# A gate projection moved into the first stage's weight tiles, and a list scheduler that keeps to one TensorE tile size

## The chip, the cores and the metric

The kernel runs on one core of a Trainium2 chip. The metric is the device time of one execution in microseconds (us); the time of a kernel is the median of its runs. The engines are TensorE (PE), VectorE (DVE), ScalarE (ACT), GpSimd (POOL), and SyncE (SP), which here does nothing but issue DMAs. In a profile's row, L62 means line 62 of the kernel; lines 62, 65, 68, 74, 77, 84 and 90 are those of small helpers (matmul, transpose, activation, scalar-tensor-tensor, tensor-tensor, copy, DMA), so a row is told by its tile names.

## What is computed

One layer of a diffusion backbone, on 512 latent tokens and a prefix of 256 context tokens, width 1024, in fp32:

```
mod = silu(c) @ w_mod + b_mod
sh1, sc1, g1, sh2, sc2, g2 = split(mod, 6)
p_lat = modulate(rmsnorm(x, norm1_g), sh1, sc1) @ w_in
p_ctx = modulate(rmsnorm(ctx, norm1_g), sh1c, sc1c) @ w_in
y = token_mixers(p_lat, p_ctx, ...)
x = x + g1 * (y @ w_out)
x = x + g2 * (relu(modulate(rmsnorm(x, norm2_g), sh2, sc2) @ w_mlp1) ** 2 @ w_mlp2)
out = rmsnorm(x, final_g)
```

`mod` has six parts of 1024 columns each, so `w_mod` is 1024 x 6144. The first two (sh1, sc1) are needed before anything else; the third, g1, the gate of the mixers' output, is needed only when `y @ w_out` is added to x. The mixers are a Mamba-2 scan (16 heads) and a gated delta rule (8 heads) in both directions; the latter inverts triangular blocks.

## The kernel before, in words

**Stage 0** (lines 220 to 355, pools `stage0` and `m0`). Eight tiles `wm` of 128 x 2048, one for each 128 rows of `w_mod`, take its first 2048 columns in two halves (`wm_load`, line 232, 512 KB each). `modrow` (line 313) multiplies them by the silu of the conditioning vectors; `silp` is padded to 32 columns, so each product uses a 128 x 32 tile of the PE array, and four of them, with four different column groups, stand side by side:

```
314          for i in range(4):
315              c0 = DM * (i // 2) + 512 * half + 256 * (i % 2)
316              mm(mps[half][32 * i:32 * i + 32, :], silp[:, k, :], wm[k][:, c0:c0 + 256], k == 0, k == KB - 1)
```

The results (`mp`) become the columns with which `hmod` (line 301) modulates the normalized and transposed x (`xtp`, `xtq`, `xT`); it leaves them as a high part `hH` and a low part `hL`.

**Projections** (`proj`, line 390). `w_in` is read in blocks of 128 columns: `sm` (small parts), then k0 g0 q0 k1 q1 k2 and so on. A block is loaded into a staging tile `st` (two buffers, `W.load`), split by ACT into `wH` and by POOL into `wL` (`W.split`, two buffers each), and multiplied with `hH` and `hL` into a PSUM tile `pl` (latent, 512 columns) and, where needed, `pc` (context, 256). Behind each block stand convolutions on ACT and DVE. `post_sm` (line 495) turns block `sm` into decay rows (`smt`, `la`, `acp`, `gcol`, `rowp`, `va`, `rowsD`), which the delta rule's four inversions (`inverse`, line 684; their products are `kk`, `qk`, `z`, `y`) read back.

**The gate** (lines 857 to 873, pool `mods`, opened behind the projection's pools). 16 tiles `mg` of 128 x 512, with three buffers, take the third 1024 columns of `w_mod` (256 KB each); two products follow each load into `gatep`, the bias `gb` is added, and four small DMAs store the row in `gD`.

**The order of the work.** The code is traced once; `_Graph` (from line 1430) knows each instruction's dependencies and a modelled duration, and `run` (line 1550) is a list scheduler. Each engine takes, of its ready instructions, the one with the lowest key, and the key is almost entirely the place in the traced code; `_keep` (line 1705) then fixes that order on every engine, SP's queue included. A PE instruction whose tile size differs from the one before is charged a little more:

```
1608              p, k = heapq.heappop(now[e])
...
1621                  if shape and shape[0] != self.shape[k][0]:
1622                      d += 45.0
```

So an instruction stands in a fixed place on its engine, and where its data come later than the model thought, everything behind it on that engine waits.

Behind the inversions come the scans (from 400 us on), the output projection (from 680 us) and the MLP (from 790 us).

Of the kernel before, what the change touches and what calls it, by code (L numbers as in the profile page):

```python
# [9 lines left out]
F32 = mybir.dt.float32  # L10
F32R = mybir.dt.float32r
AF = mybir.ActivationFunctionType
ALU = mybir.AluOpType
# [3 lines left out]
P = 128  # L17
DM = 1024
KB = DM // P
# [19 lines left out]
def tile_hybrid_ssd_gdn_dit_block(  # L39
# [6 lines left out]
    ACT, DVE, POOL, PE, SP = nc.scalar, nc.vector, nc.gpsimd, nc.tensor, nc.sync  # L46
# [3 lines left out]
    def pool(name, bufs=1, side=None, space=None, rw=None):  # L50
        kw = {}
        if side:
            kw["side"] = side
        if space:
            kw["space"] = space
        if rw:
            kw["reuse_waits"] = rw
        st = ctx.enter_context(ExitStack())
        return st.enter_context(tc.tile_pool(name=name, bufs=bufs, **kw)), st.close

    def mm(o, lhsT, rhs, start=True, stop=True):
        PE.matmul(o, lhsT=lhsT, rhs=rhs, start=start, stop=stop)  # L62
# [13 lines left out]
    def tt(o, a, b, op, eng=None):  # L76
        (eng or DVE).tensor_tensor(out=o, in0=a, in1=b, op=op)  # L77
# [11 lines left out]
    def dma(o, i, q=None):  # L89
        (q or SP).dma_start(out=o, in_=i)  # L90
# [210 lines left out]
    def hmod(k):  # L301
        if k % 2:
            act(xT[:, k, 0:LAT], xT[:, k, 0:LAT], AF.Identity, scale=Gc[:, k, 0:1], bias=modc[:, k, 0:1])
        else:
            ts(xT[:, k, 0:LAT], xT[:, k, 0:LAT], Gc[:, k, 0:1], ALU.mult, modc[:, k, 0:1], ALU.add)
        ts(xT[:, k, LAT:TOK], xT[:, k, LAT:TOK], Gc[:, k, 1:2], ALU.mult, modc[:, k, 1:2], ALU.add)
        cast(hH[:, k, :], xT[:, k, :])
        tt(hL[:, k, :], xT[:, k, :], hH[:, k, :].bitcast(F32), ALU.subtract, DVE)
# [42 lines left out]
    modcols(1)  # L351
    for k in range(4, KB):
        hmod(k)
    close_s0()
    close_m0()

# [497 lines left out]
                dma(gD[idx - 2:idx - 1, c0 - idx * DM:c0 - idx * DM + MW], br)  # L854
        done.add(f"mods{idxs[-1]}")

    md, close_md = pool("mods", side="right", rw="tile")
    gb = md.tile([P, 256], F32, name="gb")
    POOL.memset(gb, 0.0)
    for j in range(4):  # L860
        dma(gb[32 * j:32 * j + 1, :], b_mod[:, 2 * DM + 256 * j:2 * DM + 256 * j + 256])
    gp = kqt([P, 256], "gatep")
    for k in range(KB):
        for half in range(2):
            w = md.tile([P, 512], F32, tag="mw", bufs=3, name=f"mg{k}_{half}")
            c0 = 2 * DM + 512 * half
            dma(w, w_md[P * k:P * k + P, c0:c0 + 512])
            for j in range(2):
                q = 32 * (2 * half + j)
                mm(gp[q:q + 32, :], silp[:, k, :], w[:, 256 * j:256 * j + 256], k == 0, k == KB - 1)  # L870
    tt(gb, gp, gb, ALU.add)
    for j in range(4):
        dma(gD[0:1, 256 * j:256 * j + 256], gb[32 * j:32 * j + 1, :])
    go(stream(N1, D["rate"]))
    for b in range(4):
        go(inverse(b))
# [199 lines left out]

    play("mD3", "g7")
    flush()
    close_md()
    close_cw()  # L1080
    close_iw()
    bx["sd"], close_sd = pool("ssd", side="right", rw="tile")
# [34 lines left out]
    W = Weights(order)  # L1117
# [277 lines left out]
_WINDOW = 3413.4  # L1395
_SLACK = (0.0, 100.0, 100.0, 100.0, 0.0)
_LANES = 8
_MIX = 1.2e9
_STRETCH = 1.0

# [12 lines left out]
class _Graph:  # L1413
# [136 lines left out]
    def run(self, key):  # L1550
# [37 lines left out]
        while done < n:  # L1588
# [15 lines left out]
            if not now[e]:  # L1604
                if soon[e]:
                    heapq.heappush(events, (soon[e][0][0], 0, e))
                continue
            p, k = heapq.heappop(now[e])
            if self.dma[k] and len(landed) >= _LANES and landed[-_LANES] > t:
                heapq.heappush(soon[e], (landed[-_LANES] + 30.0, p, k))  # L1610
                heapq.heappush(events, (t, 0, e))
                continue
# [6 lines left out]
            elif e == 0:  # L1619
                d = self.gap[k]  # L1620
                if shape and shape[0] != self.shape[k][0]:
                    d += 45.0
                elif shape and shape != self.shape[k] and shape[2] and self.shape[k][2]:
                    d *= 0.5
                shape = self.shape[k]
# [119 lines left out]
```

## Time and profile before

| | |
|---|---|
| median of 3 runs | 1162.48 us (1159.12 to 1164.63) |
| the profiled execution | 1160.29 us, span 1158.6 us |
| PE busy | 1091.5 us, 94% of the span |
| DVE, ACT, POOL busy | 721.4, 604.0, 456.0 us |
| mean granted PE clock | 0.978 |

The profiled execution lies 2.2 us below the median. The span is the time from its first to its last instruction. PE's matmuls are pipelined: what one of them costs is read from the starts of neighbours, not from its own length.

### The profile page before, as it was taken

To read this page: it belongs to the slowest core of one execution; us is meant where nothing else is said; L and a number is where in the kernel's file an instruction comes from. 1 tells how busy PE (TensorE), PEld (TensorE's weight loads), DVE (VectorE), ACT (ScalarE), POOL (GpSimd) and SP (SyncE) were. 2 spreads that over 40 slices of the span, in tenths; PEclk is the share of its full clock that TensorE was granted. 3 is DMA by queue.
4 is the path that set the end of the run, shared out by engine and by line. 5 is a ranking of instruction groups with operands and counts; after the bars stand their busy time and mean duration, and the time that the engine had idled before them with its cause. 6 is when DMAs were issued, how large, how long until landed. Compare 5 with 4: busy or idle time off the path is not lost.

```text
span 1158.6 us, 19228 instructions
## 1 busy us (share of the span) xinstructions
PE 1091.5 (94%) x7120; PEld 885.4 (76%) x7120; DVE 721.4 (62%) x1402; ACT 604.0 (52%) x1419; POOL 456.0 (39%) x386
## 2 busy tenths in 40 slices
PE   5799998998989999999999989999999999999997
PEld 2458877787868777788878868777777888888885
DVE  3775699897979557578766777878673022444023
ACT  4647656648364577578886674125333122444133
POOL 1216444442331332222322254433545445555462
PEclk9899999999999999999999989998999999999999
DMA  9577746686564694745372277743443333333332
GB/s 313 182 198 200 229 146 185 195 227 170 157 163 146 154 347 104 267 123 207 103 273 73 92 282 237 227 136 100 137 146 109 92 107 93 91 103 98 91 104 96
DMA packets 189334, 188.44 MB, mean 163 GB/s; under 512 B 41548, under 2 KB 140153, under 8 KB 189241
## 3 DMA queue, kind: packets, MB, share of 16 engines
q1 hardware_dynamic: 188336, 186.04, 52.6%
q8 instruction: 56, 0.92, 0.3%
q10 hardware_dynamic: 905, 1.18, 0.3%
q14 instruction: 37, 0.30, 0.1%
HBM read 151.45 MB, written 35.73 MB: 162 GB/s over the span
## 4 chain that ended last, share of the span: by engine, by line
PE 70%; DVE 11%; ACT 8%; DMA 6%; issue 3%; SPq 1%; POOL 0%; ACTq 0%; DVEq 0%; POOLq 0%
PE m1p L62 15%; PE m2a L62 15%; PE wo0a L62 4%; PE wo1a L62 3%; PE pl_x L62 3%; PE pl_v L62 3%; PE pl_g L62 2%; PE yp L62 2%; PE op L62 2%; PE pc_v L62 2%; DMA st_q<-in_w_in_dram 2%; PE pp L62 2%; PE pl_z L62 2%; PE up L62 2%; PE pc_x L62 2%
## 5 line engine op out<-in xcount | busy, mean ns | idle before, releaser
L77 POOL TENSOR_TENSOR wL_m<-st_m,wH_m 128x512 fp32r<-128x512 f32 x128 | 177.4, 1405 | 186.6 <-ACT wH_m L68 177.1
L68 ACT ACTIVATE wH_m<-st_m 128x512 fp32r<-128x512 f32 x128 | 77.1, 625 | 187.0 <-PE m2a L62 111.0
L62 PE MATMUL m1p<-h2hL,wH_m 128*128 128x512 f32 (+1 forms) x272 | 104.5, 384 | 1.6 <-DVE h2hL L77 1.5
L62 PE MATMUL m1p<-h2hH,wH_m 128*128 128x512 f32 (+1 forms) x272 | 103.6, 383 | 2.5 <-ACT rl L68 2.0
L62 PE MATMUL m1p<-h2hH,wL_m 128*128 128x512 f32 (+1 forms) x272 | 103.1, 380 | 0.0
L62 PE MATMUL m2a<-wL_m,aH 128*128 128x512 f32 x256 | 99.4, 389 | 0.0
L62 PE MATMUL m2a<-wH_m,aL 128*128 128x512 f32 x256 | 99.4, 389 | 0.0
L62 PE MATMUL m2a<-wH_m,aH 128*128 128x512 f32 x256 | 98.9, 389 | 0.0
L77 DVE TENSOR_TENSOR rtmp<-m2a,g2r 128x512 f32<-128x512 f32 x16 | 10.7, 683 | 140.1 <-PE m2a L62 140.0
L77 DVE TENSOR_TENSOR rl<-rl 128x512 f32<-128x512 f32 x32 | 47.5, 1484 | 51.8 <-ACT rl L68 51.5
L62 PEld LDWEIGHTS m1p<-h2hH,wH_m 128*128 128x128 f32 x272 | 51.8, 191 | 14.0 <-ACT rl L68 4.0
L77 POOL TENSOR_TENSOR wL_wo<-st_wo,wH_wo 128x512 fp32r<-128x512 f32 x32 | 45.2, 1433 | 41.1 <-ACT wH_wo L68 35.4
L74 DVE SCALAR_TENSOR_TENSOR macc<-mw,sil,macc 128x256 f32<-128x256 f32 x84 | 56.4, 671 | 7.2 <-DMA mw<-in_w_mod_dram 5.4
L62 PEld LDWEIGHTS m1p<-h2hL,wH_m 128*128 128x128 f32 x272 | 52.1, 191 | 11.5 <-DVE h2hL L77 2.4
L77 DVE TENSOR_TENSOR TD<-YD,ND 112x30 f32<-112x30 f32 (+14 forms) x120 | 59.6, 497 | 0.9
L62 PEld LDWEIGHTS m1p<-h2hH,wL_m 128*128 128x128 f32 x272 | 52.2, 192 | 9.4
L62 PEld LDWEIGHTS m2a<-wH_m,aH 128*128 128x128 f32 x256 | 48.0, 188 | 10.1
L62 PEld LDWEIGHTS m2a<-wL_m,aH 128*128 128x128 f32 x256 | 48.0, 188 | 10.0
L62 PEld LDWEIGHTS m2a<-wH_m,aL 128*128 128x128 f32 x256 | 48.0, 188 | 9.9
L77 DVE TENSOR_TENSOR YD<-YD,TD 112x30 f32<-112x30 f32 (+14 forms) x120 | 54.5, 454 | 0.9
L665 POOL TENSOR_SCALAR_AFFINE_SELECT rw<-rw 128x512 f32<-128x512 f32 x32 | 24.0, 764 | 64.7 <-ACT er L68 60.6
L68 ACT ACTIVATE wH_wo<-st_wo 128x512 fp32r<-128x512 f32 x32 | 18.5, 623 | 50.0 <-PE wo0a L62 21.6
(496 smaller groups left out, 3224.2 us busy)
## 6 DMA issues: line engine op xcount, KB each, us to landing
st_m<-in_w_mlp_dram SPq DMA_DIRECT2D x64, 512.0 KB
wm<-in_w_mod_dram SPq DMA_DIRECT2D x16, 512.0 KB
rw<-rowsD SPq DMA_DIRECT2D x16, 512.0 KB
st_wo<-in_w_out_dram SPq DMA_DIRECT2D x16, 512.0 KB
mw<-in_w_mod_dram SPq DMA_DIRECT2D x16, 512.0 KB
Ys<-invF SPq DMA_DIRECT2D x8, 768.0 KB
st_k<-in_w_in_dram SPq DMA_DIRECT2D x8, 512.0 KB
st_g<-in_w_in_dram SPq DMA_DIRECT2D x8, 512.0 KB
```

The source lines that it names most:

```text
L62: PE.matmul(o, lhsT=lhsT, rhs=rhs, start=start, stop=stop)
L68: ACT.activation(out=o, in_=i, func=f, **kw)
L74: (eng or DVE).scalar_tensor_tensor(out=o, in0=a, scalar=s, in1=b, op0=op0, op1=op1)
L77: (eng or DVE).tensor_tensor(out=o, in0=a, in1=b, op=op)
L665: POOL.affine_select(out=rw[:, d_], in_=rw[:, d_], pattern=[[0, n], [pat, P]], compare_op=ALU.is_ge, fill=NEG, base=0, channel_multiplier=cm_)
```

## The change

Three parts. The gate's products move to the end of stage 0: its weights are loaded into the columns 0 to 1023 of the `wm` tiles, once the products of both halves with the tile are done, in eight loads of 512 KB, with four products behind each; the pool `mods` and the `mg` tiles are gone. `W.load(2)`, the load of block g0, is called ahead of the gate's loads. And the list scheduler, when the PE instruction it is about to take has another tile size than the one before, looks through the 12 lowest keys for a ready one of the same size and takes that instead (`_NEAR` is so large that it never excludes one); a switch is charged 95 instead of 45.

```diff
@@ -351,6 +351,20 @@
     modcols(1)
     for k in range(4, KB):
         hmod(k)
+
+    gb = s0.tile([P, 256], F32, name="gb")
+    POOL.memset(gb, 0.0)
+    gp = mxt([P, 256], "gatep", m0)
+    for j in range(4):
+        dma(gb[32 * j:32 * j + 1, :], b_mod[:, 2 * DM + 256 * j:2 * DM + 256 * j + 256])
+    W.load(2)
+    for k in range(KB):
+        dma(wm[k][:, 0:DM], w_md[P * k:P * k + P, 2 * DM:3 * DM])
+        for j in range(4):
+            mm(gp[32 * j:32 * j + 32, :], silp[:, k, :], wm[k][:, 256 * j:256 * j + 256], k == 0, k == KB - 1)
+    tt(gb, gp, gb, ALU.add)
+    for j in range(4):
+        dma(gD[0:1, 256 * j:256 * j + 256], gb[32 * j:32 * j + 1, :])
     close_s0()
     close_m0()
 
@@ -854,23 +868,6 @@
-    md, close_md = pool("mods", side="right", rw="tile")
-    gb = md.tile([P, 256], F32, name="gb")
-    POOL.memset(gb, 0.0)
-    for j in range(4):
-        dma(gb[32 * j:32 * j + 1, :], b_mod[:, 2 * DM + 256 * j:2 * DM + 256 * j + 256])
-    gp = kqt([P, 256], "gatep")
-    for k in range(KB):
-        for half in range(2):
-            w = md.tile([P, 512], F32, tag="mw", bufs=3, name=f"mg{k}_{half}")
-            c0 = 2 * DM + 512 * half
-            dma(w, w_md[P * k:P * k + P, c0:c0 + 512])
-            for j in range(2):
-                q = 32 * (2 * half + j)
-                mm(gp[q:q + 32, :], silp[:, k, :], w[:, 256 * j:256 * j + 256], k == 0, k == KB - 1)
-    tt(gb, gp, gb, ALU.add)
-    for j in range(4):
-        dma(gD[0:1, 256 * j:256 * j + 256], gb[32 * j:32 * j + 1, :])
     go(stream(N1, D["rate"]))
@@ -1606,6 +1603,15 @@
             p, k = heapq.heappop(now[e])
+            if e == 0 and shape and self.shape[k][0] != shape[0] and _NEAR:
+
+                for q, m in heapq.nsmallest(12, now[0]):
+                    if self.shape[m][0] == shape[0] and q < p + _NEAR:
+                        now[0].remove((q, m))
+                        now[0].append((p, k))
+                        heapq.heapify(now[0])
+                        p, k = q, m
+                        break
@@ -1619,7 +1625,7 @@
                 if shape and shape[0] != self.shape[k][0]:
-                    d += 45.0
+                    d += 95.0
```

How the order moves, at three places. First PE, where the products of the gate stood before, between the projections k0 (`pl_k_690`) and what follows; a "visit" in the text below is a run of such 32-column products with no other tile size between them:

```order
L62 MATMUL pl_k_690<-hH,wH_k_299 128x512
L62 MATMUL gatep<-mg_0_496,silp 32x256 x2
L62 MATMUL gatep<-mg_1_500,silp 32x256 x2
L62 MATMUL pl_k_690<-hL,wH_k_299 128x512
...
L62 MATMUL pl_k_690<-hL,wH_k_299 128x512
L62 MATMUL gatep<-mg_0_504,silp 32x256 x2
L62 MATMUL pl_k_690<-hH,wL_k_300 128x512
```

Of these there were 16 rows in 11 visits, the last one among the products of block q0. Now all 32 products stand in three visits, among the products of block `sm`:

```order
L62 MATMUL pl_sm<-hH,wL_sm 128x512
L62 MATMUL gatep<-wm_125,silp 32x256 x4
L62 MATMUL gatep<-wm_126,silp 32x256 x4
L62 MATMUL pl_sm<-hH,wH_sm 128x512
L62 MATMUL pc_sm<-hL,wH_sm 128x256
L62 MATMUL gatep<-wm_127,silp 32x256 x4
...
L62 MATMUL pl_sm<-hH,wL_sm 128x512
L62 MATMUL gatep<-wm_128,silp 32x256 x4
L62 MATMUL gatep<-wm_129,silp 32x256 x4
L62 MATMUL gatep<-wm_130,silp 32x256 x4
L62 MATMUL gatep<-wm_131,silp 32x256 x4
L62 MATMUL gatep<-wm_132,silp 32x256 x4
L62 MATMUL pc_sm<-hH,wL_sm 128x256
```

In the whole program PE's tile size changed 295 times before and changes 262 times now: 16 fewer by the gate, 12 fewer among the products of stage 0 (9 visits of `mp` where there were 15), 5 fewer elsewhere.

Second SP's queue, from the last load of stage 0 on (`sm`, `Abc`, `dcol` are small constants, `st_g_432` and `st_q_661` the blocks g0 and q0, `st_k_814` is k1). Before, the blocks g0 and q0 stood behind `dcol` and ahead of the gate's 16 loads; now g0 stands ahead of the gate's eight, and q0 behind them and behind the constants:

```order
L90 DMA wm_132<-in_w_mod_dram 128x2x512
L90 DMA gb<-in_b_mod_dram 1x256 x4
L90 DMA st_g_432<-in_w_in_dram 128x8x128
L90 DMA wm_125<-in_w_mod_dram 128x1024
...
L90 DMA wm_132<-in_w_mod_dram 128x1024
L90 DMA sm<-in_ssd_dt_bias_dram 16x1
...
L90 DMA dcol<-in_ssd_D_dram 64x8x1 x2
L90 DMA st_q_661<-in_w_in_dram 128x8x128
L90 DMA gD<-gb 1x256 x4
L90 DMA st_k_814<-in_w_in_dram 128x8x128
```

Third PE again, behind block q0 (`pl_q_854`; `pl_k_898` and `pc_k_899` are k1). The products and transposes that carry the decay rows, `acp`, `totp`, `rowp` and `k0t`, stood among the products of g0 before; now they stand behind all of q0, with products of k1 between them:

```order
L62 MATMUL pl_q_854<-hH,wL_q_809 128x512
L62 MATMUL pc_k_899<-hH,wH_k_846 128x256
...
L62 MATMUL acp<-la,triL 128x192
L62 MATMUL totp<-la,ones 128x384
L62 MATMUL pl_k_898<-hH,wH_k_846 128x512
L62 MATMUL pl_k_898<-hL,wH_k_846 128x512
...
L62 MATMUL pl_k_898<-hL,wH_k_846 128x512
L65 MATMUL rowp_627<-ident,gcol 64x128 x4
```

Eight products of k1 stand between `totp` and `rowp`. From here on the order differs from that of before in many places, on every engine.

## Rows read from the trace of the kernel before

**Rows 1.** The chain that ended last, by engine; then two stages.
```profile
PE 70%; DVE 11%; ACT 8%; DMA 6%; issue 3%; SPq 1%; POOL 0%; ACTq 0%; DVEq 0%; POOLq 0%
...
core 0: us, PE busy (x) PEld busy (x) DVE busy (x) ACT busy (x) POOL busy (x), PEclk, DMA share, GB/s
44.50:100.00 55.50, 51.77 (x288) 36.67 (x287) 37.57 (x66) 32.92 (x75) 16.96 (x20) 0.97 0.63 179
100.00:400.00 300.00, 279.19 (x2406) 236.49 (x2405) 245.63 (x528) 176.78 (x413) 117.00 (x104) 0.97 0.64 180
```

**Rows 2.** PE in order of time, two visits of the gate: start, length, what.
```profile
68.55 0.39 PE L62 MATMUL pl_g<-hH,wH_g 128*128 128x512 f32 x1
68.87 0.63 PE L62 MATMUL gatep<-mg,silp 128*32 128x256 f32 x4
69.42 0.50 PE L62 MATMUL pl_g<-hL,wH_g 128*128 128x512 f32 x1
69.76 0.39 PE L62 MATMUL pl_g<-hH,wL_g 128*128 128x512 f32 x1
69.99 0.39 PE L62 MATMUL pl_g<-hH,wH_g 128*128 128x512 f32 x1
...
76.12 0.64 PE L62 MATMUL gatep<-mg,silp 128*32 128x256 f32 x8
76.69 0.50 PE L62 MATMUL pl_g<-hH,wL_g 128*128 128x512 f32 x1
```

**Rows 3.** PE in order of time, two products of stage 0 without a switch.
```profile
36.58 1.94 PE L62 MATMUL mp<-wm,silp 128*32 128x256 f32 x16
```

**Rows 4.** Two short stretches, columns as in rows 1.
```profile
31.50:41.50 10.00, 7.45 (x47) 2.68 (x47) 7.34 (x10) 4.28 (x7) 2.64 (x2) 0.50 0.68 242
58.40:62.00 3.60, 3.60 (x14) 1.51 (x13) 3.26 (x5) 0.92 (x2) 0.00 (x0) 0.53 0.51 144
```

**Rows 5.** PE in order of time, three of its waits between 53 and 80 us.
```profile
55.82 0.36 PE L65 MATMUL smt<-ident,va 80*128 80x80 f32 x2 [0.62 <-ACT va L68]
58.26 1.64 PE L62 MATMUL gatep<-mg,silp 128*32 128x256 f32 x8 [1.12 <-DMA mg<-in_w_mod_dram]
74.64 0.63 PE L65 MATMUL rowp<-ident,gcol 128*64 128x128 f32 x4 [0.94 <-DVE gcol L84]
```

**Rows 6.** SP's queue in order of time, from the end of stage 0's loads.
```profile
30.40 0.45 SPq L90 DMA_DIRECT2D sm<-in_ssd_dt_bias_dram  x1
39.80 0.33 SPq L90 DMA_DIRECT2D Abc<-in_gdn_A_log_dram  x1
40.18 1.40 SPq L90 DMA_DIRECT2D dcol<-in_ssd_D_dram  x2
59.98 12.50 SPq L90 DMA_DIRECT2D mg<-in_w_mod_dram  x8
```

**Rows 7.** SP's own waits from 29 to 45 us: what, total, times, longest.
```profile
SPq L90 <- DMA wm<-in_w_mod_dram: 7.6, 8, 1.1
```

**Rows 8.** Two stretches of DMA, columns as in rows 1.
```profile
40.20:50.50 10.30, 10.30 (x73) 7.21 (x70) 6.32 (x15) 7.19 (x11) 0.32 (x1) 0.93 0.05 2
44.50:53.00 8.50, 8.50 (x47) 7.22 (x46) 7.71 (x16) 6.34 (x9) 0.08 (x1) 1.00 0.27 66
```

**Rows 9.** The chain that ended last, its piece from 42 us; start, length, what.
```profile
42.34 15.13 DMA st_q<-in_w_in_dram
```

**Rows 10.** Block q0: ACT's split, POOL's split, PE's first product.
```profile
68.68 0.63 ACT L68 ACTIVATE wH_q<-st_q 128x512 fp32r<-128x512 f32 x1 [3.61 <-PE pc_k L62]
69.39 2.85 POOL L77 TENSOR_TENSOR wL_q<-st_q,wH_q 128x512 fp32r<-128x512 f32 x2 [11.47 <-ACT wH_q L68]
83.69 0.39 PE L62 MATMUL pl_q<-hH,wH_q 128*128 128x512 f32 x1
```

**Rows 11.** Inversion 0: SP's loads of X, and PE's first product with it.
```profile
209.68 3.10 SPq L90 DMA_DIRECT2D X<-invD  x6
214.64 0.25 PE L62 MATMUL z<-X,At 32*32 32x32 f32 x4
```

More of the change, by code (lines that the diff above doesn't have):

```diff
@@ L1078, in tile_hybrid_ssd_gdn_dit_block @@
     flush()
-    close_md()
     close_cw()
@@ L1397 @@
 _LANES = 8
+_NEAR = 1e7
 _MIX = 1.2e9
```

## The prediction

> **What bounds the kernel now.** I read the chain that ended last first, then the span by stage, then PE in order of time where the gate's products stand, then SP's queue ahead of them. The chain is 70% PE [rows 1], and from 44.5 to 100 us PE is busy for 51.77 of 55.50 us, from 100 to 400 us for 279.19 of 300 [rows 1]: PE's own work bounds both stages, and between them lie 3.73 and 20.81 us in which it waits. So a microsecond of PE work that goes from a stretch where PE never rests shortens the kernel, as long as what PE does next is ready earlier too. DVE is nearest to being a second bound, with 245.63 us in the same 300 [rows 1].
>
> What the change touches, the projections of the blocks sm to q0, lies between 44.5 and 90 us. Before 44.5 us stage 0 is paced by its loads, one for each of which SP waits eight times [rows 7].
>
> **The gate's visits.** A switch of PE's tile size can be read off one visit. From the product of g0 at 68.55 to the second one behind the visit, at 69.76, 1.21 us pass [rows 2]; the two products of g0 that start in it take 0.23 us each from start to start (69.76 to 69.99), so the visit with its two switches costs 1.21 - 0.46 = 0.75 us. A visit of four products (x8, as each shows as two records) lasts 0.57 us from its start to the next instruction's, one of two products (x4) 0.55 us [rows 2]: four column groups stand side by side, and two products cost as much as four. The eleven visits of before cost 11 x 0.76 = 8.4 us. In the change there are three; the first set of four products in each costs 0.76 us, each further one what it costs without a switch. Two such sets took 1.94 us at half the clock [rows 3, 4], so about 0.49 us each at the full clock, an estimate. 3 x 0.76 + 5 x 0.49 = 4.7 us. **The gate's PE work falls by 3.7 us.** The bounds: 2.8 if a further set costs as much as the first less one switch (0.66 us), 4.6 if the sets overlap to 0.3 us.
>
> **The other switches.** Twelve fewer in stage 0 I count as nothing: the loads cover them, and if they didn't, 12 x 0.1 us more would be won. 0.1 us is a switch by the same rows: from 69.42 to 69.76 0.34 us pass against 0.23 [rows 2]. Five fewer elsewhere: 0.5 us.
>
> **PE's waits and its clock behind them.** Between 53 and 80 us PE waits 0.62 us for `va`, 1.12 us for the gate's first load, 0.94 us for `gcol` [rows 5], and the rest for `k0t`. Now `smt` stands behind products of k0, `acp` behind q0, and between `totp` and `rowp` there are eight products of k1, 8 x 0.23 = 1.8 us, twice the wait for `gcol`. I take 3.3 of the 3.73 us as gone (bounds: 1.1, the gate's load alone, to 3.7). Behind the two waits at 55 to 58 us the granted clock is 0.53 from 58.4 to 62 us [rows 4], that is, 1.2 GHz for nearly all of it; PE is busy throughout, so it loses 3.6 x 0.47 = 1.7 us of work there. With the waits I take half of that away, 0.85 us, since waits may come up elsewhere (bounds 0 and 1.7).
>
> The Trainium skill (TensorE: Matmul & The Clock Gate, section HAM oscillation) says that a kernel whose PE waits for a load ahead of each short stretch of work pays a slow start each time; by it the wait for the gate's first load would take its 1.7 us with it whole, and the sum below would be 0.85 us lower.
>
> **What the gate's new place adds.** The loads come in the same queue, SP's. SP is held eight times for a load of stage 0 [rows 7], and the rows behind them start from 30.40 to 39.80 us, 7 steps of 1.34 us [rows 6]: that is the pace of 512 KB, 390 GB/s. From 40.2 to 50.5 us the DMA engines move 2 GB/s, behind `dcol` [rows 8, 6]. The new loads go into what was this gap: the last load of stage 0 lands at about 39.8 us, block g0 behind it takes 1.34 us, the gate's eight 10.7 us; the last lands at 51.9 us. PE reaches the second group of visits when block sm's latent products are done, about when it did before, near 52.8 us, because they wait for hL; it is busy from 44.5 to 53 us without a gap [rows 8], so what the visits take there is paid by PE later, and is in the 4.7 us. I put 0.5 us of waiting there (bounds 0 and 3, the latter if the tiles come free 2 us later than I think).
>
> The Trainium skill (DMA: Bandwidth & Descriptors, section Measured) gives 78% of peak, 341 GB/s, for a load of 1 MB and less for smaller ones. By it the eight loads would take 12.3 us or more, the last would land at 53.5 us, and the wait would be 1 us longer. The rows above have 390 GB/s for 512 KB, so I keep to them.
>
> Then `Abc`, `dcol` and block q0. Before, q0 was issued at 42.34 and landed 15.13 us later, at 57.47 [rows 9], 17.7 us behind the start of the last `Abc` [rows 6]; take off 1.34 us for g0, which stood between them. Now it lands at 51.9 + 16.3 = 68.2 us, 10.7 us later than before. Was there room? ACT split q0 only at 68.68, because it waited for k0's products, and POOL's second half ended at 72.24 [rows 10], while PE wanted it at 83.69 [rows 10]. PE now comes there sooner: 83.69, less ten visits (7.6), plus the new ones (4.7), less the waits and the clock (4.2), less `acp` to `k0t`, which have moved behind (3), gives 73.6 us. The first half of wL is ready at 68.2 + 0.63 + 1.4 = 70.2 us. **No wait, with 3.4 us to spare**; bounds 0 and 2. What stands behind the split on ACT is the rest of k0's convolution and `la`, so `acp` comes late by up to 5 us, to about 77 us; PE asks for it behind q0's 24 products, at 73.6 + 5.4 = 79 us. The memsets of the inversion's tiles on DVE stand behind the gate's sum now, but ran from 52 us on before, so they move by a microsecond or two that DVE has.
>
> **The sum:** -3.7 - 0.5 - 3.3 - 0.85 + 0.5 = -7.85 us, so 1160.29 - 7.85 = 1152.4 us for the profiled execution. It lay 2.2 us under the median, so the median comes to **1154.6 us**. The change's own bounds, with the rest carried through: 1150 to 1160.
>
> **Rivals.** *The lead is lost in the inversions.* From 100 to 400 us PE's 20.81 us of waiting is for others, and the new order brings `z` of inversion 0 some 6 us of PE work further forward (the two orders counted with the durations of the trace), while DVE's elimination ahead of it moves by about 1.5 us only. PE had its first `z` at 214.64, with X's six loads issued from 209.68 on [rows 11]: there was hardly any room. If X doesn't come earlier by as much, PE waits, and what is left is what PE no longer has to do, or nothing: 0 to -4 us, 1158.5 to 1162.5. For it: DVE's load, and that the decay rows leave later than before. Against: DVE is busy for only 37.57 of 55.50 us up to 100 us [rows 1] for want of PE's results, so it will also be early.
>
> *The new order removes more waits.* If a third of the 20.81 us goes as well, 7 us: 1147.6. Nothing in the change aims at them, so it is luck of the order.
>
> *Slower: PE stands before the gate's second group.* PE's order is fixed, and all of sm's context products and k0 stand behind it. The price hangs on the pace of the loads. The slowest pace that the rows show for such loads is the gate's own, 12.50 us for eight of 256 KB [rows 6], 1.56 us each; those were also held by PE and shared with other loads. At that rate eight of 512 KB take 25 us instead of 10.7, the last lands at 66.2 us and PE waits 13.4 us instead of 0.5, with 1.7 us for the clock behind such a wait: -7.85 + 12.9 + 1.7 = +6.75, 1169.2 us. It comes out slower than before from a pace of 2.3 us for each load on, and by over 0.5% only near the bound. Against it: at 30 to 40 us nothing competes, nor will it at 40 to 52.
>
> *The scheduler's rule does nothing.* 262 switches for 295 is little; outside the gate and stage 0 it is five. That is in the sum already.
>
> **How the numbers follow.** 0.5% of 1162.48 is 5.8 us, about what a measurement of this kernel can tell from no change: faster is below 1156.7, slower above 1168.3. The forecast has 0.45 (1150 to 1160, three quarters of it below 1156.7), the lost lead 0.27, more waits gone 0.17, the gate's wait 0.11, most of it between 1162 and 1169, and a part of each goes to an order that is simply worse in the 250 us behind, which I can't read from these rows. Faster: 0.34 + 0.17 + a little of the lost lead = 0.54; slower 0.12; the same 0.34. The range that holds 8 in 10: from 1146, below the third case's middle, to 1167, within the last case's span. The forecast's own range is 1150 to 1160.
>
> **What would show it.** Right: three visits of `gatep` between 44 and 56 us, ended by 56 us, and no wait for `wm` over a microsecond; DMA busy from 40 to 52 us and then the 2 GB/s stretch; q0 landing near 68 us; PE at the first product of q0 near 74 us, of k1 near 80; no PE clock of one half between 58 and 62 us; the later milestones (first `z`, first scan, first m1p) all earlier by 6 to 9 us. Wrong: PE idle for several microseconds before `gatep` or before `pl_q`; a lead of 8 us at 100 us that is gone by 400 us; PE busy time not smaller by about 4 us.

## The result and the profile after

The changed kernel is slower: median 1172.13 us (1167.27 to 1175.68, 8 runs) against 1161.15 us for the kernel before (8 runs on the same chip), ratio 1.0094, 95% interval 1.0071 to 1.0118. That is 11 us more where 8 us less were forecast, and above the range's upper end of 1167. Its profiled execution has a span of 1168.6 us, 10.0 more than before's.

PE has a little less to do (busy 1087.3 us for 1091.5), so the time went into waits and into the clock behind them. The windows of both kernels, first before (its windows up to 100 us and of 100 to 400 us are in [rows 1]), then after; the columns are the window's length, the busy time of PE, PEld, DVE, ACT and POOL, PE's granted clock, the DMA share and GB/s:

```profile
200.00:300.00 100.00, 94.21 (x1102) 79.25 (x1102) 85.50 (x186) 66.46 (x156) 42.81 (x37) 0.98 0.70 199
770.00:805.00 35.00, 32.73 (x170) 26.64 (x170) 27.11 (x62) 16.13 (x33) 7.23 (x6) 0.90 0.34 93
```

```profile
44.50:100.00 55.50, 50.48 (x292) 39.58 (x285) 41.44 (x68) 29.48 (x55) 12.74 (x10) 0.94 0.44 135
200.00:300.00 100.00, 88.52 (x1040) 73.69 (x1039) 77.51 (x162) 61.28 (x146) 37.62 (x34) 0.93 0.66 183
400.00:680.00 280.00, 275.83 (x2186) 229.67 (x2186) 194.42 (x464) 202.00 (x583) 85.75 (x71) 0.99 0.57 185
770.00:805.00 35.00, 24.16 (x104) 17.84 (x102) 28.96 (x56) 13.40 (x26) 9.39 (x7) 0.82 0.41 116
```

Two stretches stand out. From 200 to 300 us PE waits 11.5 us instead of 5.8, at a clock of 0.93 instead of 0.98, which takes another 4.4 us (0.05 of 88.5 us busy). From 770 to 805 us it waits 10.8 us instead of 2.3.

To see when time is lost, I put the two traces beside each other by PE's progress. Each PE instruction counts with the median step of its kind in the trace of before, the gate's with nothing; the **lag** at t is how much later (or, negative, earlier) than before PE has done what before had done by t. It is used for all runs below. Where an order does its products in another sequence, it swings by some 3 us from one reading point to the next.

| lag in us at | 80 | 120 | 150 | 200 | 280 | 400 | 680 | 780 | 850 |
|---|---|---|---|---|---|---|---|---|---|
| after | -7.7 | -6.4 | -5.9 | -0.6 | 12.1 | 6.2 | 0.3 | 2.1 | 9.7 |

The lead that was forecast is there at 80 us. It is gone at 200, turns into a lag of 10 to 12 us at 280, is nearly made up by 680 us (0.3), and 7.6 us are lost right before the MLP. So most of the loss against before at the end comes from that last stretch, and what the change was to win is lost before 200 us.

**The beginning.** The gate in the changed kernel (PE in order of time; start, length, what, x for the records, two for each product):

```profile
44.19 1.07 PE L62 MATMUL gatep<-wm,silp 128*32 128x256 f32 x16
45.98 0.50 PE L62 MATMUL pl_sm<-hH,wH_sm 128*128 128x512 f32 x1 [0.71 <-ACT hH L68]
46.53 0.64 PE L62 MATMUL gatep<-wm,silp 128*32 128x256 f32 x8
47.10 0.50 PE L62 MATMUL pl_sm<-hL,wH_sm 128*128 128x512 f32 x1
...
50.24 2.37 PE L62 MATMUL gatep<-wm,silp 128*32 128x256 f32 x40
52.53 0.39 PE L62 MATMUL pc_sm<-hH,wL_sm 128*128 128x256 f32 x1
```

PE's waits between 44 and 100 us in the changed kernel (in total, times, longest):

```profile
PE pl_q L62 <- DVE cy_k L74: 2.1, 1, 2.1
PE k0t L65 <- DVE va L84: 2.1, 1, 2.1
PE pl_sm L62 <- ACT hH L68: 0.7, 1, 0.7
```

And SP's queue with the decay rows, which PE's `acp` and `rowp` end in: their store `rowsD` and their first load `rwL`, of before and then of after (issue, length):

```profile
80.04 0.50 SPq L90 DMA_DIRECT2D rowsD<-va  x1
...
82.78 0.38 SPq L90 DMA_DIRECT2D rwL<-rowsD  x1
```

```profile
37.00 5.50 SPq L90 DMA_DIRECT2D wm<-in_w_mod_dram  x8
...
51.76 0.33 SPq L90 DMA_DIRECT2D Abc<-in_gdn_A_log_dram  x1
...
88.80 0.51 SPq L90 DMA_DIRECT2D rowsD<-va  x1
...
92.70 0.38 SPq L90 DMA_DIRECT2D rwL<-rowsD  x1
```

PE is some 6 us ahead in the projections here while the decay rows leave 8.8 us later. The first step of the elimination that needs them, `TD` on DVE, starts all the same when it did (the tile's instructions, before and then after; behind the counts the shortest, median and longest in ns and the first and last start):

```profile
L77 DVE TENSOR_TENSOR TD<-YD,ND x120: 148/372/3008, 144.6 to 382.1; 112x30 f32<-112x30 f32 x8, 112x58 f32<-112x58 f32 x8, 112x84 f32<-112x84 f32 x8, 112x108 f32<-112x108 f32 x8
```

```profile
L77 DVE TENSOR_TENSOR TD<-YD,ND x120: 154/379/1467, 144.2 to 388.2; 112x30 f32<-112x30 f32 x8, 112x58 f32<-112x58 f32 x8, 112x84 f32<-112x84 f32 x8, 112x108 f32<-112x108 f32 x8
```

**The inversions.** What inversion 0 hands back comes earlier than before. X's six loads are issued at 203.49 us for 209.68 [rows 11], and PE's first `z` runs at 208.8 for 214.64, with no wait ahead of it:

```profile
203.49 3.09 SPq L90 DMA_DIRECT2D X<-invD  x6
```

PE's longest waits from 100 to 300 us in the changed kernel come behind that, `y` at 218.4 us, the two at `z` at 269.8 and 285.3:

```profile
PE z L62 <- DMA X<-invD: 3.7, 1, 3.7
PE z L62 <- issue: 3.6, 1, 3.6
PE y L62 <- issue: 3.1, 1, 3.1
```

**Before the MLP.** PE's waits from 770 to 805 us, of before and of after:

```profile
PE m1p L62 <- DVE h2hL L77: 1.5, 2, 1.2
PE m1p L62 <- DVE h2hH L84: 0.4, 1, 0.4
PE h2p L65 <- ACT h2f L68: 0.2, 1, 0.2
```

```profile
PE h2p L65 <- ACT h2f L68: 6.7, 1, 6.7
PE mrp L62 <- DVE macc L74: 4.2, 1, 4.2
```

The chain of waits there, in the changed kernel (start, length):

```profile
791.12 1.41 DVE macc L74
...
793.78 0.41 DVE br L77
...
794.21 1.07 DMA gD<-br
...
795.30 4.10 DMA mod<-gD
...
799.62 0.57 ACT h2f L68
```

These are the second modulation's two parts: DVE sums up each of eight rows in `macc`, PE folds the sum with one product `mrp` (it gives one column; the scheduler counts it as a 128x32 tile), DVE adds the bias in `br`, and the row goes through `gD` to the columns that `h2f` needs. The last row is done at 794 us; before, at 777 us. Why can be read on DVE from 700 to 795 us, before and then after:

```profile
DVE br L77 <- PE mrp L62: 1.3, 1, 1.3
```

```profile
DVE br L77 <- PE mrp L62: 9.5, 3, 7.0
```

The sum of the first row is complete at 724.7 us, but its `mrp` runs at 731.10, behind full-size products of `wo0a`: the rule takes any of them first, as long as one is ready. DVE's next sums wait behind `br`.

### The profile page after: what moved, and what is told of

It reads as the page before. It is cut to its first block, busy times and chain, and to the rows that moved or that the text cites. A ratio compares the mean times of both kernels' runs of the same rounds, so it can differ in the third digit from the quotient of the medians.

```text
span 1168.6 us, 19219 instructions
## 1 busy us (share of the span) xinstructions
PE 1087.3 (93%) x7120; PEld 888.7 (76%) x7120; DVE 724.8 (62%) x1402; ACT 607.2 (52%) x1421; POOL 461.0 (39%) x386
## 4 chain that ended last, share of the span: by engine, by line
PE 68%; DVE 16%; DMA 6%; ACT 5%; issue 3%; SPq 1%; POOL 1%; ACTq 0%; POOLq 0%; DVEq 0%
PE m1p L62 15%; PE m2a L62 15%; PE pl_x L62 4%; PE pl_z L62 3%; DVE TD L77 3%; PE wo0a L62 3%; PE wo1a L62 2%; PE op L62 2%; PE yp L62 2%; DVE YD L77 2%; PE pp L62 2%; DVE cy_v L74 2%; DMA wm<-in_w_mod_dram 2%; PE pc_x L62 2%; PE up L62 2%
## 5 line engine op out<-in xcount | busy, mean ns | idle before, releaser
L77 DVE TENSOR_TENSOR TD<-YD,ND 112x30 f32<-112x30 f32 (+14 forms) x120 | 63.3, 527 | 9.7 <-issue 8.4
L74 DVE SCALAR_TENSOR_TENSOR macc<-mw,sil,macc 128x256 f32<-128x256 f32 x84 | 59.5, 708 | 6.2 <-DMA mw<-in_w_mod_dram 4.5
L77 POOL TENSOR_TENSOR wL_x<-st_x,wH_x 128x512 fp32r<-128x512 f32 x16 | 21.0, 1326 | 69.4 <-ACT wH_x L68 53.0
L77 DVE TENSOR_TENSOR aL<-rl,aH 128x512 fp32r<-128x512 f32 x32 | 30.3, 947 | 18.9 <-ACT aH L68 18.8
```

Source lines behind the costliest of these rows:

```text
L74: (eng or DVE).scalar_tensor_tensor(out=o, in0=a, scalar=s, in1=b, op0=op0, op1=op1)
```

## The experiments

**Theory A**: the rule loses the 8 us before the MLP, because it holds back `mrp`. **Theory L**: the orders behind the change are simply other draws of the list scheduler, and the one of before is a good one; from e5 on it says more, that the gate's new place is worth what was forecast and only the new orders lose it. Against them **rival 1** of the prediction (the lead is lost in the inversions), from e5 on as **theory I** (the inversions can't start earlier, whatever the order), later as **theories D and K**, by which the decay rows set the pace.

### The rule and the gate apart (e1 to e4, e6)

e1, `mrp` exempt from the rule:

```diff
-            if e == 0 and shape and self.shape[k][0] != shape[0] and _NEAR:
+            if e == 0 and shape and self.shape[k][0] != shape[0] and _NEAR and (2 * k < self.n or self.shape[k][0] != (128, 32)):
```

> The changed kernel with one exception from the scheduler's new rule: the eight products mrp of the second modulation weights (and those of the last part) are taken when their turn comes, though their tile is 128x32. PE's order is the changed kernel's up to the output projection. Theory A (the rule holds these products back, the sums on DVE and the rows that h2 needs come late, and PE waits 4.2 + 6.7 us for them before the MLP): the two waits go, the first m1p comes some 8 us earlier, and the time is about 1160 to 1163 us on a chip where before takes 1161, that is 0 to +2 us against before. Rival B (the tail is late only because everything before it is late): no more than 2 us won, 1169 to 1172.

e6, the kernel before with the rule for `mrp` alone:

```diff
+            if e == 0 and shape and self.shape[k][0] != shape[0] and 2 * k > self.n and self.shape[k][0] == (128, 32):
+                for q, m in heapq.nsmallest(12, now[0]):
...
```

> The kernel before with the rule for the eight products mrp of the second modulation weights alone (those of the last part too); the order is the same as before's up to the output projection. Theory A: PE waits before the MLP as in the changed kernel, the first m1p comes 5 to 9 us later, 1166 to 1170 us. Rival B: the tail was late for other reasons, within 2 us of before.

e1: 1166.67 us, ratio 1.005 (1.0026 to 1.0075). e6: 1168.92 us, ratio 1.0052 (1.0029 to 1.0074). PE's waits from 770 to 805 us, e1 and then e6:

```profile
PE m1p L62 <- DVE h2hL L77: 1.5, 2, 1.2
PE m1p L62 <- DVE h2hH L84: 0.4, 1, 0.4
```

```profile
PE h2p L65 <- ACT h2f L68: 6.7, 1, 6.7
PE mrp L62 <- DVE macc L74: 4.4, 1, 4.4
```

Without the rule on these eight products the two waits go, and with the rule on nothing else they come, in a program whose order is before's up to the output projection. From 780 to 850 us e1 loses nothing (lag 11.9 to 11.6) and e6 7.2 us (0.2 to 7.4), for 7.6 in the changed kernel. Theory A is shown for these waits, and e6 has the price that it gave. But e1 lies in neither of its two ranges: it is still 0.5% slower than before, so the rest of its loss comes from the gate and the order. (e1's profile was 4 to 9 us later than the changed kernel's from 280 to 780 us, with the same order up to the output projection: single profiles differ by that much, so verdicts are taken from the ratios.)

e2 (the gate's new place, without rule and with the charge 45), e3 (rule and charge 95, the gate in its old place) and e4 (the change with the rule off):

```diff
-            if e == 0 and shape and self.shape[k][0] != shape[0] and _NEAR:
...
-                    d += 95.0
+                    d += 45.0
```

> The gate's new place alone; the scheduler as in the kernel before (no rule, a switch charged 45). Theory A: mrp's products stand as in the kernel before, so the tail loses nothing. If the new place is worth what was forecast for it and the rule alone loses it in the inversions, the time is 1153 to 1157 us; rival C, that the gate's new place itself makes the order of 200 to 300 us worse (a block of the projection moved forward, kk of the last inversion moved back by 33 us of PE work), gives 1160 to 1164, with a lead of 4 us or more at 150 us that is gone by 300 us.

> The scheduler's rule and the charge of 95 alone; the gate where it was before. Theory A: the tail loses some 8 us as in the changed kernel, and nothing is won at 50 to 80 us: 1166 to 1172 us. If the rule were harmless and the loss came with the gate's place: 1159 to 1163.

> The changed kernel with the rule off (the number behind it zero) and the charge of 95 kept. Theory A: mrp's products stand where they stood before, no waits of 4.2 and 6.7 us before the MLP. If the rule also spoils the inversions: 1152 to 1157 us. If the gate's place spoils them (rival C): 1160 to 1164 us.

| | us | ratio | lag at 80 | 150 | 280 | 400 | 680 | 780 | 850 |
|---|---|---|---|---|---|---|---|---|---|
| e2 gate only | 1173.97 | 1.0118 (1.0082 to 1.0154) | -5.5 | -8.3 | 3.1 | -2.1 | 7.9 | 9.9 | 9.8 |
| e3 rule only | 1169.04 | 1.0077 (1.0050 to 1.0104) | -0.5 | -1.4 | 5.3 | -1.8 | -5.5 | 0.5 | 7.4 |
| e4 rule off | 1170.57 | 1.0079 (1.0044 to 1.0114) | -4.5 | -5.3 | 8.3 | 2.5 | 6.7 | 11.0 | 10.0 |

e3 came out as theory A had it: the rule alone costs what the tail costs. e2 and e4, the gate without the rule, are slower than either of their ranges. e2 has its lead up to 150 us, no loss in the tail, and is the slowest of the three: it loses 11 us by 280 us and again 10 us between 400 and 680 us. Of the second loss no run shows the cause; PE's longest wait there is 3.9 us.

### Other orders without the change (e7, e8, e17)

```diff
-                    d += 45.0
+                    d += 95.0
```

e8 has 46 instead of 95; e17 is the changed kernel with 96 instead of 95.

> The kernel before with the charge for a switch of 95 in place of 45, and nothing else: the scheduler makes another order from 30 us on. Theory L (the order of the kernel before is a good one among many, and nearly any new one loses some us somewhere): 4 to 10 us slower than before, 1165 to 1171, though not one instruction was added or taken away. If the losses come from the gate's move or from the rule: within 3 us of before.

> The kernel before with the charge 46 in place of 45, a change of 1 ns in the model; some 280 PE rows stand elsewhere, the first of them before 60 us. Theory L: 2 to 8 us slower, 1163 to 1169. If orders differ little in worth: within 2 us of before.

> The changed kernel with a charge of 96 in place of 95; PE's order is the same up to row 1194 (behind 150 us) and differs in some 220 rows behind it. Theory L (what an order wins or loses behind 150 us is chance of a few us): the tail's 8 us stay, the lag at 300 us comes out otherwise than the changed kernel's 9.8 us by 3 or more, the time anywhere from 1163 to 1174. If the lag at 300 us belongs to the rule or the gate: within 2 us of the changed kernel.

e7: 1162.95 us, ratio 1.0012 (0.9990 to 1.0034). e8: 1155.75 us, ratio 0.995 (0.9927 to 0.9972). e17: 1170.11 us, ratio 1.0073 (1.0050 to 1.0096). Theory L falls as I had put it: e7 is the same as before, and e8 is faster by 5.8 us, outside both of its ranges. Orders do differ by some 6 us of chance. These are only two other orders, so chance isn't excluded for any one kernel; but five orders with the gate in its new place (the changed kernel, e1, e2, e4, e17) are slower by 0.5 to 1.2%, and neither of these two is. And e17, whose order is nearly the changed kernel's, has its lags at 200 and 280 us again (-0.3 and 11.9).

So **before with a charge of 46 beats both kernels**; its profile is ahead from 680 to 700 us on (lag -2.7 to -5.0), where PE waits 1.7 us for `yhL` instead of 2.4 for `yhH`.

### The gate moved, everything else in before's order (e5, e9, e10, e11)

The order of before is planned first, its start times become the keys, and only the gate's instructions get new ones:

```diff
+        if gate_new[k]:
+            when[k] = new.when[k]
+        else:
...
+            when[k] = old.when[rest[j]]
+            j += 1
```

> The gate moved as in the change (eight loads behind stage 0, three visits), and every other instruction on each engine in the order of the kernel before; only the loads sm, Abc and dcol stand behind the gate's loads, block g0 ahead of them, and PE's smt behind the third visit. It takes the scheduler's reshuffling out of the change. Theory L (the gate's new place is worth what was forecast, and the new orders of the 250 us behind it lose it): a lead of 5 to 8 us at 100 us that is still 4 us or more at 300 and at the end, so 1153 to 1157 us where before takes 1161. Theory I (the inversions can't start earlier, whatever the order, since what they wait for is not earlier): the lead is gone by 300 us and the time is 1158 to 1162. PE's waits for acp and gcol stay in either case, as their places are those of before; that is some 1 to 2 us less than the forecast.

> As the run before it of the gate in before's order, but up to q0's block (90 us of the model) every engine takes the order that the scheduler makes for the gate's new place, so that neither the exponential of Abc on ACT nor the memsets on DVE stand in the way (they cost the last one 8.9 us and 10.2 us of PE waits); behind it, from PE's row 216 on, the order is exactly before's on each engine. Theory L: a lead of 5 us or more at 100 us that is still at least 3 us at 300 and at the end: 1154 to 1158 us where before takes 1162. Theory I: the lead is gone by 300 us, 1160 to 1163. The last one's lag stayed between 11.4 and 15.7 us from 80 us to the end, so what is lost early isn't made up; if the same holds for what is won, L is right.

> The same with the new order up to 75 us of the model only, so that PE's acp, totp and rowp stand where they stood before, between g0 and q0, with no gate's visits ahead of them to cover DVE's chain of the decay rows. Both theories: PE waits 2 to 6 us for la there, the lead at 100 us is 2 to 5 us smaller than with 90. Theory L: 1156 to 1162; theory I: 1160 to 1165.

> The gate in its new place as in the run with 90, on top of the order that the charge 46 makes (1155.75 us where before took 1162.3, ratio 0.995). Theory L: both gains add, 1148 to 1153 us. Theory I: the same as with 46 alone, 1154 to 1158.

| | us | ratio | lag at 80 | 120 | 200 | 400 | 680 | 850 |
|---|---|---|---|---|---|---|---|---|
| e5 | 1176.53 | 1.0132 (1.0102 to 1.0163) | 14.7 | 13.0 | 12.5 | 11.4 | 14.7 | 15.6 |
| e9 | 1163.66 | 1.0017 (0.9991 to 1.0043) | -4.3 | 2.2 | 1.9 | -1.2 | 3.7 | 5.5 |
| e10 | 1164.28 | 1.0031 (1.0006 to 1.0056) | -3.2 | 3.7 | 3.5 | -0.3 | 3.4 | 4.4 |
| e11 | 1160.93 | 0.9997 (0.9971 to 1.0022) | -4.4 | 6.8 | 5.5 | 5.8 | 6.2 | 5.4 |

e5 was spoilt by my splice at its start: ACT stood at the exponential of `Abc`, whose load is now behind the gate's, and DVE's memsets ahead of the decay rows waited for the gate's sum. It is outside both of its ranges and shows one thing: a lag of 14.7 us at 80 us is one of 11 to 16 us from there to the end. In this order nothing is made up later. In e9 and e11 a lead of 4 to 7 us at 80 to 100 us is gone at 120 us, in e10 one of 3 us at 80 us is gone at 100. Of theory I's ranges (1160 to 1163 for e9, 1160 to 1165 for e10) e10 meets its own and e9 misses its own by 0.7 us; e11 is above both of its ranges. PE's longest wait between 44 and 110 us in e9, and POOL at that time:

```profile
PE pl_q L62 <- POOL wL_q L77: 8.3, 1, 8.3
```

```profile
93.13 0.77 POOL L680 TENSOR_SCALAR_AFFINE_SELECT rwC<-rwC 128x256 f32<-128x256 f32 x2 [6.95 <-issue]
...
102.00 1.27 POOL L77 TENSOR_TENSOR wL_q<-st_q,wH_q 128x512 fp32r<-128x512 f32 x1
```

The same low half in before:

```profile
100.05 1.31 POOL L77 TENSOR_TENSOR wL_q<-st_q,wH_q 128x512 fp32r<-128x512 f32 x1
```

On POOL the low half of q1's weights stands behind the masks of the decay rows, and those wait for the rows' loads. So it is ready 2 us later than before, while PE is there 6.6 us sooner. This is a lead lost in the way that rival 1 has it, since what PE does next isn't ready earlier, but not at rival 1's place: it is lost to the decay rows on POOL, more than 100 us ahead of the first `z`. On the order of charge 46 the same move loses the 0.5% that this order had won.

### What the decay rows hold (e12 to e16, e18)

Theory D: the rows are late because `Abc` now lands behind the gate's loads. ACT waits 6.19 us for it ahead of `va`, and DVE's seven memsets stand between; `ua` starts at 64.73 us (60.53 before). e12 moves `Abc`'s two instructions and the memsets in the changed kernel, e13 in e9, e14 in the kernel before:

```diff
+    when[find(2, "Abc", "Abc")[0]] = when[find(2, "ea", "ea")[0]] + 1.0
+    when[find(1, "Abc", "Abc")[0]] = after - 1.0
...
+        when[k] = late + 2500.0 * (j + 1)
```

> The changed kernel in its own order, with nine instructions moved: on ACT the exponential of Abc stands behind ea's instead of ahead of va, on DVE the product of Abc stands just ahead of the one that needs it, and the seven memsets of the inversions' tiles stand behind the decay rows (two to three us apart). PE, POOL and SP are as in the change. Theory D (the small load Abc, which now lands behind the gate's eight loads, holds va on ACT and the memsets on DVE, so the decay rows come 4 to 8 us late and with them the inversions): acp, which came at 79.3 us, can't come before PE has done q0's products, but PE has acp's data ready then, rowp and the store of the decay rows come 1 to 4 us earlier, the lag of up to 12 us at 280 us falls by 3 to 8 us, and the time is 1164 to 1169 us, 8 of the tail being still in it. Rival M (the lag at 280 us comes from the order of the products and loads there, not from the decay rows): within 2 us of the changed kernel, 1170 to 1174.

> The gate in its new place with before's order behind 90 us of the model, and the same nine instructions moved. Here PE waited 8.29 us at 95 us for the second half of q1's low part, which stands on POOL behind the decay rows' masks. Theory D: the rows reach POOL 4 to 6 us earlier, that wait falls to 2 to 4 us or goes, the lead at 120 us is 2 to 6 us, it stays to 650 us, and the time is 1155 to 1160 us where before takes 1161.5. Rival M: the wait stays over 6 us and the time within 2 us of 1163.7.

> The kernel before with the same instructions moved and nothing else; the gate is in its old place. The decay rows can come up to 3 us earlier (the memsets held ua from 57.4 to 60.5 us). Theory D: PE's order holds the gate's visits ahead of acp, rowp and q0, so PE itself is hardly earlier: 0 to -3 us, 1158 to 1162. If the decay rows are the whole bound of what follows: -3 to -5 us.

e12: 1172.08 us, ratio 1.0091 (1.0059 to 1.0123), the same as the changed kernel. e13: 1163.66, ratio 1.0014 (0.9989 to 1.0038), the same as e9. e14: 1163.29, ratio 1.0012 (0.9986 to 1.0038). Theory D falls: the rows are stored 1.9 us earlier in e12 (86.9), which is within what it gave, and neither the lag at 280 us nor the time moves. That speaks against the rows as the pace in the changed kernel's own order, too. In e13 they are 0.7 us earlier (82.2 for 82.9). `ua`, 4.2 us late in the changed kernel, is still 1.9 us late in e12 (62.4). By the traces that rest is lost ahead of `Abc` (no run takes it apart): `smt`, which begins their chain, needs block sm's context products, and PE does those behind the gate's third visit (first `smt` at 58.2 us, 54.0 before, 59.3 in e12). Most of what the 8.8 us have besides comes where PE takes `acp` behind all of q0's products. In the old place the gate's products ran in the time in which ACT and DVE worked on this chain.

e15 moves the low half on POOL ahead of the masks, e16 does it on the order of charge 46:

```diff
+    when[low[3]] = when[low[2]] + 1.0
```

> As the last run of the gate in its new place with before's order behind, and one more instruction moved: on POOL the second half of q1's low part stands right behind the first, ahead of the masks of the decay rows, which wait for the rows' loads until 94.9 us. PE waited 10.9 us for it at 94 us. Theory Q (that one place on POOL loses the lead): the wait goes, PE passes q1 and k2 with its lead, and waits at kk of the first inversion by no more than 2 us; lead of 5 us or more at 120 us, kept to the end: 1154 to 1158 us. Rival R (what follows hangs on the decay rows all the same, since kk's results, the masks and the elimination need them, and the rows are no earlier than before's): the wait turns up again at kk or at the y and z of the first inversion, at most 3 us are left at 220 us, 1158 to 1162.

> The same on the order of the charge 46, which alone took 0.995 of before's time. Theory Q: 1147 to 1152 us. Rival R: 1152 to 1156, no better than with 46 alone.

e15: 1166.92 us, ratio 1.0034 (1.0014 to 1.0054). e16: 1162.03, ratio 0.9995 (0.9973 to 1.0016). Both are slower than their two ranges. Rival R was right that nothing is won, but not where: it looked for the wait at `kk`, `y` and `z`. PE's wait in e15, and ACT at that time:

```profile
PE pl_k L62 <- DVE cy_k L74: 9.9, 1, 9.9
```

```profile
93.29 0.99 ACT L68 ACTIVATE rwC<-rwC,bc 128x128 f32<-128x128 f32 x3 [4.98 <-POOL rwC L680]
...
100.39 0.67 ACT L68 ACTIVATE cy_k<-pl_k,gcw 128x512 f32<-128x512 f32 x1
```

The wait turns up one block further on: k1's convolution stands on ACT behind the scaling of the rows, and PE can't have k1's accumulator for k2 before it.

e18 does the reverse. It leaves the gate alone and the rest of before's order, and makes the decay rows late; `k0t`, the transposes of k0, move with them:

```diff
+    for k in find(0, "acp") + find(0, "totp") + find(0, "rowp") + [k for k in range(graph.n) if graph.eng[k] == 0 and _name(graph.ins[k].outs[0]).startswith("k0t")]:
+        when[k] += 8500.0
```

> The kernel before, gate and order as they were, but PE takes acp, totp, rowp and k0t some 8 us of its own work later (between the last products of g0 and those of q0), so that the decay rows are stored 6 to 9 us later, as in the changed kernel (88.8 us there, 80.0 before). No work is added but some eight switches, under 1 us, and PE has products to do in the meantime. Theory K (the decay rows set the pace of what follows, so a lead in the projections is worth nothing and their lateness is paid): PE waits 4 to 8 us between 90 and 130 us, the lag at 130 us is 4 to 8 us and stays, 1165 to 1170 us. Rival N (the rows have room): within 2 us of before.

1170.79 us, ratio 1.0087 (1.0057 to 1.0117). The rows' store, PE's longest waits from 90 to 135 us, and the masks on POOL and q1's high half on ACT, all in e18:

```profile
87.10 0.50 SPq L90 DMA_DIRECT2D rowsD<-va  x1
```

```profile
PE pl_q L62 <- POOL wL_q L77: 2.5, 1, 2.5
PE pl_q L62 <- ACT wH_q L68: 1.7, 1, 1.7
```

```profile
95.75 0.77 POOL L665 TENSOR_SCALAR_AFFINE_SELECT rwC<-rwC 128x256 f32<-128x256 f32 x2 [9.22 <-DMA rwC<-rowsD]
```

```profile
102.66 0.61 ACT L68 ACTIVATE wH_q<-st_q 128x512 fp32r<-128x512 f32 x1
```

The same two in before:

```profile
90.47 0.77 POOL L665 TENSOR_SCALAR_AFFINE_SELECT rwC<-rwC 128x256 f32<-128x256 f32 x2 [3.94 <-DMA rwC<-rowsD]
```

```profile
97.43 0.62 ACT L68 ACTIVATE wH_q<-st_q 128x512 fp32r<-128x512 f32 x1
```

The rows are 7.1 us late. The masks on POOL, and on ACT the scaling of the rows behind them, stand waiting for the rows' loads; q1's weights stand behind these on both engines, 5.2 us late, and PE waits for both halves. PE's lag is 0.4 us at 80, 5.8 at 120 and 6.1 at 850 us. Theory K is shown for before's order: PE is not behind at 100 us, and what the rows are late is paid for at once and is still there at the end. Two things stay open: of the median's 10 us the profiled execution, 4.4 us below that median, has only 6.1, and the move of `k0t` was not tried apart from that of the rows, though the waits in the trace are for the rows.

## Why the prediction was wrong

**Right.** The gate's PE work: three visits of 1.07, 0.57 and 2.29 us (the first by its own length, as a wait follows it), 3.9 us, and with 0.19 us for the switch behind each, as in the forecast's 0.76, 4.5 us for 4.7. So it falls by 3.9 where 3.7 was put (bounds 2.8 to 4.6), and PE's busy time by 4.2; a further set costs (2.29 - 0.57) / 4 = 0.43 us for the estimated 0.49. The gate's loads: no wait for `wm`. q0's load was there at 66.5 us at the latest (68.2 forecast), `acp` ran at 79.3 (79), k1 at 80.3 (80), PE's lead at 80 us is 7.7. The DMA engines moved 383 GB/s from 40.2 to 50.5 us, so the rows' pace of 390 held. The 341 GB/s of the Trainium skill (DMA: Bandwidth & Descriptors, section Measured) are for one load of 1 MB that GpSimd issues; the measured 383 GB/s, for 512 KB loads one behind the other on SP's queue, are more.

**Wrong in size.** "The waits, -3.3": PE waits 5.02 us between 44.5 and 100 us, for 3.73 before. The three that I had named are gone, but PE comes to q0 at 69.5 instead of 73.6 and waits 2.15 us for k0's convolution, and 2.1 us for the decay rows' `va`. "No wait, with 3.4 us to spare" asked only for q0's weights, not for the accumulator that k0's convolution had to empty first. "The half clock, -0.85": it is gone from 58.4 to 62 us (granted 1.00, 0.53 before [rows 4]), and the wait ahead of it is gone with it. The Trainium skill (TensorE: Matmul & The Clock Gate, section HAM oscillation) says that a slow start behind such a wait comes back with each one; this trace agrees, with 1.00 for 0.53. But behind the new waits the half clock came back, and the stretch as a whole has 0.94 for 0.97, some 1.5 us lost where 0.85 was to be won.

**The step that failed first** is the sum's own condition, "as long as what PE does next is ready earlier too". I asked it of q0 and of `acp`, and of nothing behind them. In before's order the runs show what it misses: q1's weights stand on POOL and ACT behind the decay rows, so they come no earlier (2 us later in e9) while PE comes 6.6 us sooner, and the lead is gone within 20 us by a wait of 8.3 us. Late rows, with `k0t` moved along, cost 0.9% there (e18). In the changed kernel's own order the place is another: the lead, 7.7 us at 80 and 5.9 at 150 us, is gone at 200, and PE is 12 us behind at 280.

Rival 1 got 0.27 and had that place nearly right, but not the mechanism. It says that X comes no earlier; X comes 6 us earlier, the lead is all but gone by then, and the waits come behind it, at `y` and at later `z`. Its time, 1158.5 to 1162.5, was also too good, since it stopped at a lost lead. That the rows leave 8.8 us later, which it named for itself, doesn't hold up the first `z`.

**The step that was missing** is the rule's price beyond switches. "262 switches for 295 is little; outside the gate and stage 0 it is five" counted what the rule saves and not whom it keeps waiting: eight products, each with a chain on DVE behind it, 7.2 us (e6). The sum put this term at nothing ("That is in the sum already"); by the lags it is 7.6 of the 9.7 us that the changed kernel loses against before.

The rival that came out slower, a wait for the gate's loads, had nothing to do with it, and "a part of each goes to an order that is simply worse" was not priced; the orders of e7 and e8, from no change to 5.8 us faster, show that orders differ by that much, not what a worse one costs.

**Open**: of the changed kernel's lead that goes by 200 us, and of its 12 us between 200 and 280 us, the place is shown (for the latter waits at `y`, `z` and the clock behind them), not the cause. Earlier rows don't move it (e12), nor does another charge (e17); both keep nearly the changed kernel's order. e4, without the rule, has 8.3 us at 280 us too, so which part of the change makes it isn't shown. The chain can't simply be put ahead of the gate either: by the program's pools the tile `va`, its first step, lies in memory that stage 0 gives back, so it comes behind the gate's last product. Giving it other memory wasn't tried.

## What to carry to other kernels

Ask of work that is moved what it was covering where it stood: products that fill PE while a chain runs on other engines cost little of what they seem to there, and put ahead of the chain's first step they can delay all that stands behind the chain on any engine with a fixed order (shown here in before's order), even if PE never waits for the chain itself. A lead on one engine is worth nothing unless each thing that it needs next is earlier too. A rule that saves switches should exempt short products on which another engine's chain depends; count whom it delays, not only what it saves. And with a list scheduler, run the same work under one or two neighbouring charges before believing in 0.5%: a charge of 46 for 45 was worth 0.5% here.

## What the runs showed that was not expected

The waits before the MLP cost what they last, and not the clock on top. In the changed kernel PE waits 4.2 and 6.7 us there, and the granted clock is 0.51 behind them, that is nearly all at 1.2 GHz. But in before, without the two waits, it is 0.75 in the same window, that is about half of it at 1.2 GHz, with PE busy for almost all of it. After and then before (PE alone: length, busy time, granted clock, DMA share and GB/s):

```profile
792.50:806.00 13.50, 6.75 (x28) 0.51 0.40 101
```

```profile
792.50:806.00 13.50, 12.98 (x81) 0.75 0.35 98
```

At half the clock go 0.49 of 6.75 us in the one, 3.3 us, and 0.25 of 12.98 us in the other, 3.2 us. So what the changed kernel loses there is the 6.75 us in which PE stands idle, for 0.52 before.

And a lag that is there at 120 us in before's order is there at 850 us within 3.3 us in these profiles (e5, e9, e10, e11, e18), though single profiles of one order lie up to 5 us from its median. That is no property of the work: in the changed kernel's order a lag of 12 us at 280 us is down to 0.3 at 680.
